# Value products of two heads alternate in one group per step, and the causal mask moves into the scan

## The chip, the cores and the metric

The kernel runs on one core of one Trainium2 chip. TensorE (PE, with its weight loads shown as PEld), VectorE (DVE), ScalarE (ACT), GpSimd (POOL) and the DMA queues work side by side and wait for each other through semaphores. The metric is the device time of one run in microseconds (us). The median of three runs of the kernel before is 3113.42 us (3112.48 to 3114.47).

## The reference

Two blocks follow each other on a sequence of 1024 rows with 1024 features. The first block has two layers (window attention, then a gated linear recurrence, each with memory attention and a wide MLP); nothing of it is touched. The second block has 8 stick-breaking heads and 8 sliding-window heads, each of width 64, between an input projection and an output projection. What the change touches is this part of the reference:

```
for start in range(0, S, BLOCK):            # BLOCK = 128 queries
    end = start + BLOCK
    z = einsum('bqhd,bkhd->bhqk', q[:, start:end], k[:, :end]) * scale
    causal = kpos < qpos
    log_beta = log_sigmoid(z)
    log_1mb = where(causal, log_sigmoid(-z), 0.0)
    later = cumsum(log_1mb, axis=3, reverse=True) - log_1mb
    w = where(causal, exp(log_beta + later), 0.0)
    outs.append(einsum('bhqk,bkhd->bqhd', w, v[:, :end]))
```

So the weight of key s for query t is sigmoid(z_ts) times the product of sigmoid(-z_tj) over the keys j between s and t, and zero for s at or after t.

## The kernel before, in words

The second block works on features in the partitions. `Piece.half` (L1147) computes one projected piece of 128 features for one half of the sequence: 24 matmuls of 128x512 into a PSUM bank `pj` of the tag "mm", which has two banks. The piece is then evacuated by ACT and DVE.

The 8 stick-breaking heads go in four pairs; the two heads of a pair (j = 0 and 1) lie in partitions 0 to 63 and 64 to 127. For each pair there are eight steps n = 0 to 7, one for each block of 128 queries, and step n has n + 1 blocks of keys. The loop is at L1291 to L1301. One turn of it writes down, in this order, the scores of step n + 1 (`sb_a`), one half of a projection that a later pair needs (`pc.half`), and the values of step n (`sb_b`).

`sb_a` (L1178): for each chunk of up to 512 keys and each head, three matmuls (L1193) that use 64 rows of the array, into a PSUM bank `z` of the tag "S", which has three banks. In the chunk that holds the diagonal a fourth matmul (L1196, bf16) adds a large negative number at keys that are not before the query. ACT makes `om` = sigmoid(-z/8) (L1197) and `be` = sigmoid(z/8) (L1198). DVE runs a product scan over `om` from the last key to the first (L1201), and `be` is multiplied by the scan shifted by one key (L1204; DVE for head 0, POOL for head 1). `be` has four buffers, which is two steps, and `om` has two, which is one step.

`sb_b` (L1207) takes one head after the other. For each head and each group of up to four key blocks it transposes `be` on PE (L1217) into a bank of the tag "tr" (two banks), copies it to an SBUF tile `wt` (three buffers; L1220 DVE for the first group, L1222 ACT for the second), and multiplies each block with the values (L1224): 128 rows, 64 columns of the array, output in `po` at partitions 64j to 64j + 63. So the products of head 0 occupy the array's columns 0 to 63 and those of head 1 columns 64 to 127. Each such product is two matmul instructions in the trace: 288 products, 576 instructions. `stage_out` (L1165) then multiplies with the gate and stores.

The sliding-window heads follow (L1304 to L1315) with `sw_a` and `sw_b` (L1253). `sw_b` handles two query blocks in one `po`; for each block it transposes and copies both heads together, then multiplies (L1271) the two key blocks of head 0 and the two of head 1.

The order of instructions on each engine is fixed when the program is built: the tile framework plays the program forward with assumed durations and takes, on each engine, the earliest written instruction whose inputs and buffers are there. `ahead(n)` (L94) makes it treat the instructions inside as if they had been written n instructions earlier. On the chip each engine then runs its list in that order and waits where a semaphore is not there yet.

Of the kernel before, what the change touches and what calls it, by code (L numbers as in the profile page):

```python
# [10 lines left out]

F32 = mybir.dt.float32
F32R = mybir.dt.float32r
BF16 = mybir.dt.bfloat16
I32 = mybir.dt.int32
AF = mybir.ActivationFunctionType
ALU = mybir.AluOpType
# [5 lines left out]
P = 128  # L23
D = 1024
S = 1024
# [5 lines left out]
NEG = -1e30  # L31
# [13 lines left out]


@with_exitstack
def net_kernel(ctx: ExitStack, tc: tile.TileContext, xT, memT, vecs, pos, sinks, invf, mask0, maskc, alibi,
               w_memk, w_memv, w_attn, w_mq, w_out, w_up, w_down, w_lru, w_gate, w_in2, w_out2, w_ada, outT):
    nc = tc.nc  # L50
    pe, act, dve, pool = nc.tensor, nc.scalar, nc.vector, nc.gpsimd

    cp = ctx.enter_context(tc.tile_pool(name="cp", bufs=1))
# [15 lines left out]
    psp = Tags(ctx.enter_context(tc.tile_pool(name="ps", bufs=1, space=PSUM)), {"mm": 2, "S": 3, "tr": 2, "po": 1})  # L69
# [13 lines left out]
    def nm(base):  # L83
        n_name[0] += 1
        return f"{base}_{n_name[0]}"

    ident = cp.tile([P, P], F32, tag="ident", name="ident")
# [356 lines left out]
    with tc.tile_pool(name="s0", bufs=1) as tp, \  # L444
# [19 lines left out]
        for l in range(2):  # L464
# [15 lines left out]
            for q in range(4):  # L480
                wh, wl = weight(w_memv[l * 4 + q])
                nc.sync.dma_start(xs[4 + q][:, hs(l)], xT[:, 4 + q, hs(l)])
                for m in range(2):
                    mm3(pss[m], [(memh[:, 2 * q + k, m * P:m * P + P], meml[:, 2 * q + k, m * P:m * P + P],
                                  wh[:, k * 512:k * 512 + 512], wl[:, k * 512:k * 512 + 512]) for k in range(2)],
                        start=q == 0, stop=q == 3)
# [47 lines left out]
    with ExitStack() as ph:  # L534
        a0, pre = side_pool(ph, "a0", "left"), ph.enter_context(ExitStack())
        a0r = side_pool(pre, "a0r", "right")
        T = Tags({"row": a0r, "rs": a0r, "ta": a0r, "tb": a0r, None: a0}, {"q": 12, "st": 12, "pt": 4, "mP": 1})
        gs = {}

        def proj_a(g, t):  # L540
            if g not in gs:
                gs[g] = ([weight(w_attn[g * 4 + q], 768) for q in range(4)],
                         T.tile([P, 2, S], F32R, "ks", nm("ks")), T.tile([P, NB, HD], F32, "vr", nm("vr")), [])
            ws, ks, vr, qs = gs[g]
# [3 lines left out]
                               ws[k // 2][1][:, (k % 2) * 384:(k % 2) * 384 + 384]) for k in range(KC)])  # L548
            row = T.tile([P, 384], F32, "row", nm("row"))
            act.copy(row, ps[:, :384])  # L550
# [3 lines left out]
            rsw = row[:, :320].rearrange("p (h a e) -> p h a e", a=8, e=8)[:, :, :2, :][:, :, ::-1, :]  # L554
            ta = T.tile([P, 5, 16], F32, "ta", nm("ta"))
            tb = T.tile([P, 5, 16], F32, "tb", nm("tb"))
# [300 lines left out]
    for l in range(2):  # L857
        if l == 1:

            with ExitStack() as ph:  # L860
# [3 lines left out]
                le = side_pool(lru, "a1", "left")  # L864
                T = Tags({"xb": ra, "xch": ra, "xcl": ra, "gl": rb, None: le},
                         {"xch": 1, "xcl": 1, "sq": 1, "i": 3, "r": 3})
# [99 lines left out]
                for c in range(KC):  # L966
# [3 lines left out]
                    ri = lru_g(c, cc[1], cc[2])  # L970
# [142 lines left out]
        down = ctx.enter_context(ExitStack())  # L1113


    identb = cp.tile([P, P], BF16, tag="identb", name="identb")
    dve.tensor_copy(identb, ident)
    mskc = cp.tile([P, P], BF16, tag="mskc", name="mskc")
    mskf = cp.tile([P, P], F32, tag="mskf", name="mskf")
    nc.scalar.dma_start(mskf, maskc)  # L1120
    dve.tensor_copy(mskc, mskf)
    with ExitStack() as ph:
        ri = ph.enter_context(tc.tile_pool(name="a2r", bufs=1, side="right", reuse_waits="tile"))
        le = side_pool(down, "a2", "left")
        T = Tags({"qkh": ri, "qkl": ri, "vr": ri, None: le}, {"qkh": 4, "qkl": 4, "be": 4, "st": 8, "wt": 3})

        def proj(w, th):
            wh, wl = w
# [49 lines left out]
        def sb_a(pc, n):  # L1178
            (qh, ql), (kh, kl) = pc[0].t, pc[1].t
            nk = (n + 1) * P  # L1180
            qs_ = slice(n * P, n * P + P)
            bes = [T.tile([P, S], F32, "be", nm("be")) for _ in range(2)]
            oms = [T.tile([P, S + 1], F32, "om", nm("om")) for _ in range(2)]
            for j in range(2):
                pool.memset(oms[j][:, nk:nk + 1], 1.0)
            for k0 in range(0, nk, 512):
                w = min(512, nk - k0)
                diag = k0 + w == nk
                zs = [psp.tile([P, 512], F32, tag="S", name=nm("z")) for _ in range(2)]
                for i, (a, b) in enumerate(((qh, kh), (qh, kl), (ql, kh))):  # L1190
                    for j in range(2):
                        rs_ = slice(64 * j, 64 * j + 64)
                        pe.matmul(zs[j][:, :w], a[rs_, qs_], b[rs_, k0:k0 + w], start=i == 0, stop=i == 2 and not diag)  # L1193
                for j in range(2):
                    if diag:
                        pe.matmul(zs[j][:, w - P:w], identb, mskc, start=False, stop=True)  # L1196
                    act.activation(oms[j][:, k0:k0 + w], zs[j][:, :w], AF.Sigmoid, scale=-0.125)  # L1197
                    act.activation(bes[j][:, k0:k0 + w], zs[j][:, :w], AF.Sigmoid, scale=0.125)  # L1198
            for j in range(2):
                be, om = bes[j], oms[j]  # L1200
                dve.tensor_tensor_scan(out=om[:, :nk][:, ::-1], data0=om[:, :nk][:, ::-1],  # L1201
                                       data1=om[:, :nk][:, ::-1], initial=1.0, op0=ALU.mult, op1=ALU.bypass)
                e = pool if j else dve
                e.tensor_tensor(out=be[:, :nk], in0=be[:, :nk], in1=om[:, 1:nk + 1], op=ALU.mult)  # L1204
            return bes

        def sb_b(pc, n, bes, st, chunk):  # L1207
            vr, sg = pc[2].t, pc[3].t
            po = psp.tile([P, HT], F32, tag="po", name=nm("po"))
            for j in range(2):  # L1210
                rs_ = slice(64 * j, 64 * j + 64)
                be = bes[j]
                for k0 in range(0, n + 1, 4):
                    kn = min(4, n + 1 - k0)
                    pt = psp.tile([P, 512], F32, tag="tr", name=nm("wtr"))
                    for b in range(kn):
                        pe.transpose(pt[:, b * P:b * P + P], be[:, (k0 + b) * P:(k0 + b + 1) * P], ident)  # L1217
                    wt = T.tile([P, 512], F32, "wt", nm("wt"))
                    if k0 == 0:
                        dve.tensor_copy(wt[:, :kn * P], pt[:, :kn * P])  # L1220
                    else:
                        act.copy(wt[:, :kn * P], pt[:, :kn * P])  # L1222
                    for b in range(kn):
                        pe.matmul(po[rs_, :P], vr[:, k0 + b, rs_], wt[:, b * P:b * P + P],  # L1224
                                  start=k0 + b == 0, stop=k0 + b == n, skip_group_check=True)
            stage_out(st, po, sg, chunk, n, P)

        def sw_a(pk, pq, c, n0, alb):
# [24 lines left out]
        def sw_b(pv, pg, c, n0, p, st):  # L1253
            vr, sg = pv.t, pg.t
            po = psp.tile([P, HT], F32, tag="po", name=nm("wpo"))
            for nn in range(2):
                n = n0 + nn
                k0 = max(0, n - 1)
                kb = n + 1 - k0
                pt = psp.tile([P, 512], F32, tag="tr", name=nm("swt"))  # L1260
                for j in range(2):
                    for b in range(kb):
                        o = (j * kb + b) * P
                        pe.transpose(pt[:, o:o + P], p[:, 2 * nn + j, b * P:b * P + P], ident)  # L1264
                wt = T.tile([P, 512], F32, "wt", nm("swp"))
                (act.copy if nn else dve.tensor_copy)(wt[:, :2 * kb * P], pt[:, :2 * kb * P])
                for j in range(2):
                    rs_ = slice(64 * j, 64 * j + 64)
                    for b in range(kb):
                        o = (j * kb + b) * P  # L1270
                        pe.matmul(po[rs_, nn * P:nn * P + P], vr[:, k0 + b, rs_], wt[:, o:o + P],  # L1271
                                  start=b == 0, stop=b == kb - 1, skip_group_check=True)
            stage_out(st, po, sg, 4 + c, n0, 256)

        KINDS = ("split", "split", "rows", "gate")
# [15 lines left out]
        for p in range(4):  # L1291
            st = [None, None]
# [11 lines left out]
        for c in range(4):  # L1304
            st = [None, None]
# [62 lines left out]
def layout(**inp):  # L1368
    a = {k: np.asarray(v) for k, v in inp.items()}
    o = {}  # L1370
# [13 lines left out]
    qi = np.arange(P)[:, None]  # L1384
    rel = np.arange(3 * P)[None, :] - P - qi
    o["mask0"] = np.where(np.abs(rel) <= 128, 0.0, 8 * NEG).astype(np.float32)
    o["maskc"] = np.where(np.arange(P)[None, :] < qi, 0.0, 8 * NEG).astype(np.float32)
    rel2 = P + qi - np.arange(2 * P)[None, :]
    tabs = []
    for c in range(4):  # L1390
# [39 lines left out]
    for c in range(4):  # L1430
# [6 lines left out]
    return {k: np.ascontiguousarray(v) for k, v in o.items()}  # L1437


ORDER = ("xT", "memT", "vecs", "pos", "sinks", "invf", "mask0", "maskc", "alibi", "w_memk", "w_memv", "w_attn", "w_mq",  # L1440
         "w_out", "w_up", "w_down", "w_lru", "w_gate", "w_in2", "w_out2", "w_ada")


# [17 lines left out]
```

## Time and profile before

| | |
|---|---|
| runs | 3113.42 us median of 3 (3112.48 to 3114.47) |
| profiled execution | 3114.57 us, its span 3112.6 us |
| granted TensorE clock, mean over the span | 0.981 |
| busy | PE 2994.6 us (96%), DVE 1803.7 (58%), ACT 1300.7 (42%), POOL 391.9 (13%) |
| stick-breaking stage | scores first at 2468.8 us, values last at 2892.3 us |

The busy time of an engine is the union of its instructions. Matmuls overlap in the array: a row that begins 0.23 us after the one before can still last 0.39 us. So how fast a group of matmuls passes is read from the starts, or from the length of a whole group, and not from the mean duration of one.

### The profile page before, as it was taken

How to read it: one execution, taken by the hardware profiler on the slowest of the kernel's cores; microseconds unless marked ns; L12 is line 12 of the kernel's file. 1: busy time of each engine (PE TensorE's matmuls, PEld its weight loads, DVE VectorE, ACT ScalarE, POOL GpSimd, SP SyncE). 2: the span in 40 equal slices, each digit the busy share in tenths (PEclk: the TensorE clock that was granted, in tenths of full speed). 3: DMA queues.
4: the chain of work that ended last, by engine and by line, in shares of the span. 5: the costliest groups of instructions: out<-in, count | busy, mean ns of one | idle time of the engine just before them, and what ended most of it. 6: DMA issues, size and time to landing. Idle time of an engine off the chain costs nothing. (4 is left out here: it accounts for less than half of the span.)

```text
span 3112.6 us, 38989 instructions
## 1 busy us (share of the span) xinstructions
PE 2994.6 (96%) x14688; PEld 2430.1 (78%) x14688; DVE 1803.7 (58%) x3071; ACT 1300.7 (42%) x2390; POOL 391.9 (13%) x426
## 2 busy tenths in 40 slices
PE   8999999799999999999889889999999899999998
PEld 7888778678888888777667768888888677777777
DVE  8666754774456542788764674445243745555555
ACT  6566541544542221366751444451121433334442
POOL 3222100300000000243310300000001201111102
PEclk9999999999999999999999989999999899999999
DMA  7111354343365432221263333354231210111142
GB/s 265 36 55 55 101 194 150 125 149 102 108 215 194 143 115 71 68 68 65 78 254 139 119 129 109 109 181 151 68 123 54 81 55 35 35 35 48 62 176 75
DMA packets 136348, 341.61 MB, mean 110 GB/s; under 512 B 14944, under 2 KB 29664, under 8 KB 136160
## 3 DMA queue, kind: packets, MB, share of 16 engines
q1 hardware_dynamic: 131840, 331.93, 31.1%
q10 hardware_dynamic: 4320, 7.20, 0.7%
q8 instruction: 115, 1.88, 0.2%
q14 instruction: 73, 0.60, 0.1%
HBM read 245.22 MB, written 93.85 MB: 109 GB/s over the span
## 5 line engine op out<-in xcount | busy, mean ns | idle before, releaser
L122 PE MATMUL psd<-uh,wh 128*128 128x512 f32 (+1 forms) x1568 | 606.2, 387 | 2.5 <-DVE mql L105 1.7
L126 PE MATMUL psd<-uh,wl 128*128 128x512 f32 (+1 forms) x1568 | 606.5, 387 | 0.0
L125 PE MATMUL psd<-ul,wh 128*128 128x512 f32 (+1 forms) x1568 | 606.3, 387 | 0.0
L104 ACT CAST wh<-wr 128x1024 fp32r<-128x1024 f32 (+2 forms) x236 | 234.7, 998 | 730.6 <-PE psd L125 506.3
L105 DVE TENSOR_TENSOR wl<-wr,wh 128x1024 fp32r<-128x1024 f32 (+2 forms) x260 | 314.4, 1212 | 218.1 <-ACT wh L104 216.9
L316 DVE TENSOR_TENSOR x<-x,psd 128x512 f32<-128x512 f32 x288 | 196.1, 685 | 377.7 <-PE psd L126 372.6
L122 PEld LDWEIGHTS psd<-uh,wh 128*128 128x128 f32 x1568 | 294.6, 188 | 63.8 <-issue 2.3
L126 PEld LDWEIGHTS psd<-uh,wl 128*128 128x128 f32 x1568 | 294.6, 188 | 60.7 <-issue 2.6
L125 PEld LDWEIGHTS psd<-ul,wh 128*128 128x128 f32 x1568 | 294.6, 188 | 59.7 <-issue 1.7
L122 PE MATMUL psu<-oph,wh 128*128 128x512 f32 x512 | 200.4, 394 | 41.1 <-ACT wh L104 41.1
L154 POOL TENSOR_TENSOR acc<-acc,sq 128x512 f32<-128x512 f32 (+1 forms) x70 | 95.8, 1369 | 1009.5 <-ACT sq L150 998.3
L125 PE MATMUL psu<-opl,wh 128*128 128x512 f32 x512 | 199.8, 391 | 0.0
L126 PE MATMUL psu<-oph,wl 128*128 128x512 f32 x512 | 198.6, 390 | 0.0
L125 PE MATMUL pj<-hl,wh 128*128 128x512 f32 x416 | 166.1, 404 | 8.0 <-DVE hl L105 8.0
L122 PE MATMUL pj<-hh,wh 128*128 128x512 f32 x416 | 168.4, 409 | 2.5 <-DVE qkl L105 1.3
L126 PE MATMUL pj<-hh,wl 128*128 128x512 f32 x416 | 167.0, 406 | 0.0
L122 PEld LDWEIGHTS psu<-oph,wh 128*128 128x128 f32 x512 | 96.6, 189 | 62.4 <-ACT wh L104 42.0
L125 PEld LDWEIGHTS psu<-opl,wh 128*128 128x128 f32 x512 | 96.7, 189 | 20.3 <-issue 0.5
L126 PEld LDWEIGHTS psu<-oph,wl 128*128 128x128 f32 x512 | 96.6, 189 | 20.3
L1201 DVE TENSOR_TENSOR_SCAN om<-om 128x128 f32<-128x128 f32 (+7 forms) x64 | 86.0, 1352 | 38.5 <-ACT om L1197 38.3
L122 PE MATMUL psx<-hh,wh 128*128 128x512 f32 x256 | 99.0, 397 | 4.8 <-ACT gl L897 4.8
L122 PE MATMUL psu<-oph,vh 128*128 128x512 f32 x256 | 100.7, 393 | 0.0
(337 smaller groups left out, 6027.9 us busy)
## 6 DMA issues: line engine op xcount, KB each, us to landing
wr<-in_w_up SPq DMA_DIRECT2D x64, 512.0 KB, 3.8
ud<-cc SPq DMA_DIRECT2D x128, 256.0 KB, 2.2
ur<-ud SPq DMA_DIRECT2D x64, 512.0 KB, 3.4
wr<-in_w_down SPq DMA_DIRECT2D x64, 512.0 KB, 4.1
wr<-in_w_out SPq DMA_DIRECT2D x32, 512.0 KB, 3.6
wr<-in_w_in SPq DMA_DIRECT2D x26, 512.0 KB, 3.5
wra<-in_w_ada SPq DMA_DIRECT2D x24, 512.0 KB, 4.3
uh<-mixh SPq DMA_DIRECT2D x20, 512.0 KB, 7.6
```

The source lines that it names most:

```text
L104: act.copy(hi, src)
L105: lo_eng.tensor_tensor(out=lo, in0=src, in1=hi.bitcast(F32), op=ALU.subtract)
L122: ins = pe.matmul(out, lh, rh, start=start and i == 0, stop=False, skip_group_check=skip)
L125: pe.matmul(out, lh, rl, start=False, stop=False, skip_group_check=skip)
L126: ins = pe.matmul(out, ll, rh, start=False, stop=stop and i == n - 1, skip_group_check=skip)
L154: pool.tensor_tensor(out=self.acc[:, :n], in0=self.acc[:, :n], in1=sq[:, :n], op=ALU.add)
L316: dve.tensor_tensor(out=xs, in0=xs, in1=ps, op=ALU.add)
L1201: dve.tensor_tensor_scan(out=om[:, :nk][:, ::-1], data0=om[:, :nk][:, ::-1], data1=om[:, :nk][:, ::-1], initial=1.0, op0=ALU.mult, op1=ALU ...
```

## The change

Four edits. The mask matmul, its two constants and the input that it came from go; the scan gets a second operand `turns` that is zero but for an identity matrix in the diagonal block, and adds it after the multiplication, from 0 at the start: the running product is 0 before the diagonal, becomes 1 at it and is multiplied from there on. The element beyond the last key is set to 0 and not 1. The second chunk's scores of head 1 use a bank of the tag "mm" and not "S". In `sb_b` all transposes and copies of a step come first (the copies of head 0 on DVE, of head 1 on ACT, `wt` now with five buffers), and then all products of both heads in one group, from the last key block to the first, the heads alternating, written 200 instructions ahead. `sw_b` is turned the same way.

```diff
-        T = Tags({...}, {"qkh": 4, "qkl": 4, "be": 4, "st": 8, "wt": 3})
+        T = Tags({...}, {"qkh": 4, "qkl": 4, "be": 4, "st": 8, "wt": 5, "turns": 1})
+        turns = T.tile([P, S], F32, "turns", nm("turns"))
+        pool.memset(turns[:, :S - P], 0.0)
+        pool.tensor_copy(turns[:, S - P:], ident)
...
-                pool.memset(oms[j][:, nk:nk + 1], 1.0)
+                pool.memset(oms[j][:, nk:nk + 1], 0.0)
...
-                zs = [psp.tile([P, 512], F32, tag="S", name=nm("z")) for _ in range(2)]
+                zs = [psp.tile([P, 512], F32, tag="mm" if k0 and j else "S", name=nm("z")) for j in range(2)]
...
-                    if diag:
-                        pe.matmul(zs[j][:, w - P:w], identb, mskc, start=False, stop=True)
...
-                                       data1=om[:, :nk][:, ::-1], initial=1.0, op0=ALU.mult, op1=ALU.bypass)
+                                       data1=turns[:, S - nk:][:, ::-1], initial=0.0, op0=ALU.mult, op1=ALU.add)
...  sb_b
-            for j in range(2):
-                for k0 in range(0, n + 1, 4):
...
-                    for b in range(kn):
-                        pe.matmul(po[rs_, :P], vr[:, k0 + b, rs_], wt[:, b * P:b * P + P],
-                                  start=k0 + b == 0, stop=k0 + b == n, skip_group_check=True)
+            for k0 in range(0, n + 1, 4):
+                for j in range(2):
...
+                    (act.copy if j else dve.tensor_copy)(wt[:, :kn * P], pt[:, :kn * P])
+                    wts.append(wt)
+            with ahead(200):
+                for b in range(n, -1, -1):
+                    for j in range(2):
+                        rs_ = slice(64 * j, 64 * j + 64)
+                        pe.matmul(po[rs_, :P], vr[:, b, rs_], wts[b // 4 * 2 + j][:, b % 4 * P:b % 4 * P + P],
+                                  start=b == n, stop=b == 0, skip_group_check=True)
...  sw_b
+            with ahead(200):
+                for nn in (1, 0):
+                    wt, k0, kb = wts[nn]
                     for b in range(kb):
-                        o = (j * kb + b) * P
+                        for j in range(2):
+                            o = (j * kb + b) * P
```

## Rows read from the trace of the kernel before

**Rows 1.** Page, busy time of the engines and busy tenths in 40 slices.
```profile
PE 2994.6 (96%) x14688; PEld 2430.1 (78%) x14688; DVE 1803.7 (58%) x3071; ACT 1300.7 (42%) x2390; POOL 391.9 (13%) x426
...
PE   8999999799999999999889889999999899999998
```

**Rows 2.** Busy time by stretch: start:end us, length, busy us (instructions), clock, DMA share.
```profile
2460.00:2895.00 435.00, 433.59 (x2300) 321.96 (x2300) 243.78 (x370) 165.68 (x360) 51.88 (x102) 0.99 0.13 43
2895.00:3113.00 218.00, 205.62 (x1266) 164.56 (x1264) 117.17 (x339) 89.17 (x223) 36.42 (x50) 0.97 0.31 109
```

**Rows 3.** Chain that ended last, stretch 2460 to 2895 us, shares by line.
```profile
by line: PE pj L122 17.4%; PE pj L126 17.2%; PE pj L125 17.2%; PE po L1224 15.7%; PE z L1193 14.7%; PE wtr L1217 9.1%; PE z L1196 2.1%; PE vtr L1158 1.2%; issue 1.2%; PE ws L1243 1.0%; POOL hr L252 0.8%; ACT hr L260 0.5%; DVE qkl L105 0.4%;
```

**Rows 4.** Groups by line, whole run: count | busy us, mean ns | idle before, releaser.
```profile
L1224 PE MATMUL po<-wt,vr 128*64 128x128 f32 x576 | 73.0, 279 | 0.0
L1217 PEld LDWEIGHTS wtr<-ident,be 128*128 128x128 f32 x288 | 31.7, 140 | 10.9 <-issue 9.1 <-DVE be L1204 0.4
L1196 PE MATMUL z<-mskc,identb 128*128 128x128 bf16 x64 | 13.8, 229 | 0.0
L1271 PE MATMUL wpo<-swp,vr 128*64 128x128 f32 x240 | 18.2, 283 | 0.0
```

**Rows 5.** PE in order of time: start us, us of the group, line, tiles, count.
```profile
2526.72 0.44 PE L1224 MATMUL po<-wt,vr 128*64 128x128 f32 x4
...
2636.64 0.66 PE L1224 MATMUL po<-wt,vr 128*64 128x128 f32 x8
...
2678.95 1.09 PE L1224 MATMUL po<-wt,vr 128*64 128x128 f32 x8
...
2701.12 0.39 PE L122 MATMUL pj<-hh,wh 128*128 128x512 f32 x1
2701.35 0.39 PE L125 MATMUL pj<-hl,wh 128*128 128x512 f32 x1
2701.67 1.96 PE L1224 MATMUL po<-wt,vr 128*64 128x128 f32 x16
...
2910.36 1.14 PE L1271 MATMUL wpo<-swp,vr 128*64 128x128 f32 x16
```

**Rows 6.** Groups by line and shape: the scores of 512 keys, first of three terms.
```profile
L1193 PE MATMUL z<-qkh,qkh 64*128 64x512 f32 x48 | 21.8, 495 | 0.0
```

**Rows 7.** PE in order of time: scores of two heads together, and of one head.
```profile
2643.32 0.50 PE L1193 MATMUL z<-qkh,qkh 64*128 64x512 f32 x2
2643.66 0.40 PE L1193 MATMUL z<-qkl,qkh 64*128 64x512 f32 x2
2643.89 0.41 PE L1193 MATMUL z<-qkh,qkl 64*128 64x512 f32 x2
2644.14 0.28 PE L1193 MATMUL z<-qkh,qkh 64*128 64x256 f32 x1
...
2711.68 0.49 PE L1193 MATMUL z<-qkh,qkh 64*128 64x512 f32 x1
2712.01 0.39 PE L1193 MATMUL z<-qkl,qkh 64*128 64x512 f32 x1
2712.24 0.39 PE L1193 MATMUL z<-qkh,qkl 64*128 64x512 f32 x1
2712.57 0.23 PE L1196 MATMUL z<-mskc,identb 128*128 128x128 bf16 x1
2712.61 0.47 PE L125 MATMUL pj<-hl,wh 128*128 128x512 f32 x1
```

**Rows 8.** Waits, stretch 2460 to 2895 us: us in total, times, longest us.
```profile
ACT be L1198 <- PE wtr L1217: 46.6, 16, 5.9
```

**Rows 9.** Groups by line and shape: copies to `wt` and the longest scan, 2460 to 2895 us.
```profile
L1220 DVE COPY wt<-wtr 128x512 f32<-128x512 f32 x40 | 27.4, 685 | 33.6 <-PE wtr L1217 33.4
L1201 DVE TENSOR_TENSOR_SCAN om<-om 128x1024 f32<-128x1024 f32 x8 | 18.3, 2290 | 7.4 <-ACT om L1197 7.4
L1222 ACT COPY wt<-wtr 128x512 f32<-128x512 f32 x8 | 4.7, 586 | 21.9 <-PE wtr L1217 21.9
```

**Rows 10.** A scan in the first block that multiplies and adds: count, ns min/median/max, start us.
```profile
L947 DVE TENSOR_TENSOR_SCAN r<-a,i x8: 2274/2277/2283, 1347.6 to 1575.9; 128x1024 f32<-128x1024 f32 x8
```

More of the change, by code (lines that the diff above doesn't have):

```diff
@@ L13 @@
 F32R = mybir.dt.float32r
-BF16 = mybir.dt.bfloat16
 I32 = mybir.dt.int32
@@ L47, in net_kernel @@
 @with_exitstack
-def net_kernel(ctx: ExitStack, tc: tile.TileContext, xT, memT, vecs, pos, sinks, invf, mask0, maskc, alibi,
+def net_kernel(ctx: ExitStack, tc: tile.TileContext, xT, memT, vecs, pos, sinks, invf, mask0, alibi,
                w_memk, w_memv, w_attn, w_mq, w_out, w_up, w_down, w_lru, w_gate, w_in2, w_out2, w_ada, outT):
@@ L1113, in net_kernel @@
         down = ctx.enter_context(ExitStack())
[L1116 to L1121, printed above, removed]
     with ExitStack() as ph:
@@ L1124, in net_kernel @@
         le = side_pool(down, "a2", "left")
-        T = Tags({"qkh": ri, "qkl": ri, "vr": ri, None: le}, {"qkh": 4, "qkl": 4, "be": 4, "st": 8, "wt": 3})
+        T = Tags({"qkh": ri, "qkl": ri, "vr": ri, None: le}, {"qkh": 4, "qkl": 4, "be": 4, "st": 8, "wt": 5, "turns": 1})
+        turns = T.tile([P, S], F32, "turns", nm("turns"))
+        pool.memset(turns[:, :S - P], 0.0)
+        pool.tensor_copy(turns[:, S - P:], ident)
         def proj(w, th):
@@ L1184, in sb_a @@
             for j in range(2):
-                pool.memset(oms[j][:, nk:nk + 1], 1.0)
+                pool.memset(oms[j][:, nk:nk + 1], 0.0)
             for k0 in range(0, nk, 512):
                 w = min(512, nk - k0)
-                diag = k0 + w == nk
-                zs = [psp.tile([P, 512], F32, tag="S", name=nm("z")) for _ in range(2)]
+                zs = [psp.tile([P, 512], F32, tag="mm" if k0 and j else "S", name=nm("z")) for j in range(2)]
                 for i, (a, b) in enumerate(((qh, kh), (qh, kl), (ql, kh))):
@@ L1192, in sb_a @@
                         rs_ = slice(64 * j, 64 * j + 64)
-                        pe.matmul(zs[j][:, :w], a[rs_, qs_], b[rs_, k0:k0 + w], start=i == 0, stop=i == 2 and not diag)
+                        pe.matmul(zs[j][:, :w], a[rs_, qs_], b[rs_, k0:k0 + w], start=i == 0, stop=i == 2)
                 for j in range(2):
-                    if diag:
-                        pe.matmul(zs[j][:, w - P:w], identb, mskc, start=False, stop=True)
                     act.activation(oms[j][:, k0:k0 + w], zs[j][:, :w], AF.Sigmoid, scale=-0.125)
@@ L1209, in sb_b @@
             po = psp.tile([P, HT], F32, tag="po", name=nm("po"))
-            for j in range(2):
-                rs_ = slice(64 * j, 64 * j + 64)
-                be = bes[j]
-                for k0 in range(0, n + 1, 4):
-                    kn = min(4, n + 1 - k0)
+            wts = []
+            for k0 in range(0, n + 1, 4):
+                kn = min(4, n + 1 - k0)
+                for j in range(2):
                     pt = psp.tile([P, 512], F32, tag="tr", name=nm("wtr"))
                     for b in range(kn):
-                        pe.transpose(pt[:, b * P:b * P + P], be[:, (k0 + b) * P:(k0 + b + 1) * P], ident)
+                        pe.transpose(pt[:, b * P:b * P + P], bes[j][:, (k0 + b) * P:(k0 + b + 1) * P], ident)
                     wt = T.tile([P, 512], F32, "wt", nm("wt"))
[L1219 to L1222, printed above, removed]
-                    for b in range(kn):
-                        pe.matmul(po[rs_, :P], vr[:, k0 + b, rs_], wt[:, b * P:b * P + P],
-                                  start=k0 + b == 0, stop=k0 + b == n, skip_group_check=True)
+                    (act.copy if j else dve.tensor_copy)(wt[:, :kn * P], pt[:, :kn * P])
[6 more added lines that the diff above has]
+                                  start=b == n, stop=b == 0, skip_group_check=True)
             stage_out(st, po, sg, chunk, n, P)
@@ L1255, in sw_b @@
             po = psp.tile([P, HT], F32, tag="po", name=nm("wpo"))
+            wts = []
             for nn in range(2):
@@ L1266, in sw_b @@
                 (act.copy if nn else dve.tensor_copy)(wt[:, :2 * kb * P], pt[:, :2 * kb * P])
-                for j in range(2):
-                    rs_ = slice(64 * j, 64 * j + 64)
+                wts.append((wt, k0, kb))
+            with ahead(200):
+                for nn in (1, 0):
+                    wt, k0, kb = wts[nn]
                     for b in range(kb):
-                        o = (j * kb + b) * P
-                        pe.matmul(po[rs_, nn * P:nn * P + P], vr[:, k0 + b, rs_], wt[:, o:o + P],
-                                  start=b == 0, stop=b == kb - 1, skip_group_check=True)
+                        for j in range(2):
+                            rs_ = slice(64 * j, 64 * j + 64)
+                            o = (j * kb + b) * P
+                            pe.matmul(po[rs_, nn * P:nn * P + P], vr[:, k0 + b, rs_], wt[:, o:o + P],
+                                      start=b == 0, stop=b == kb - 1, skip_group_check=True)
             stage_out(st, po, sg, 4 + c, n0, 256)
@@ L1386, in layout @@
     o["mask0"] = np.where(np.abs(rel) <= 128, 0.0, 8 * NEG).astype(np.float32)
-    o["maskc"] = np.where(np.arange(P)[None, :] < qi, 0.0, 8 * NEG).astype(np.float32)
     rel2 = P + qi - np.arange(2 * P)[None, :]
@@ L1437, in layout @@
     return {k: np.ascontiguousarray(v) for k, v in o.items()}
-ORDER = ("xT", "memT", "vecs", "pos", "sinks", "invf", "mask0", "maskc", "alibi", "w_memk", "w_memv", "w_attn", "w_mq",
+ORDER = ("xT", "memT", "vecs", "pos", "sinks", "invf", "mask0", "alibi", "w_memk", "w_memv", "w_attn", "w_mq",
          "w_out", "w_up", "w_down", "w_lru", "w_gate", "w_in2", "w_out2", "w_ada")
```

## The prediction

> **What bounds the kernel now.** I read the page's busy times first: PE is busy for 96% of the span, and the slices of the second block (the last quarter) show it at 9 tenths throughout [rows 1]. A busy PE isn't yet a PE at its peak, so the next view is the busy time by stretch. The stick-breaking stage runs from 2460 to 2895 us. PE is busy for 433.6 of its 435 us at a granted clock of 0.99, DVE for 243.8 (56%), ACT for 165.7 and POOL for 51.9 [rows 2]. The reader is to see that PE has no gap here and that no other engine is near its limit. The third view is the chain that ended last in this stretch: 52% of it are projections (three rows of 17%), 15.7% the value products, 14.7% the scores, 9.1% the transposes and 2.1% the mask matmuls; no other engine has more than 1% [rows 3]. So in this stage a microsecond that PE doesn't need is a microsecond off the span, as long as the other engines keep up. In the transposes, PE waited for `be` for 0.4 us in all [rows 4]: the scan and its multiplication are done long before they are needed. In the last 218 us PE is busy for 205.6 [rows 2], so what is won before 2895 us isn't waited away behind it.
>
> **The products.** The 576 product instructions take 73.0 us together [rows 4]. How fast a group passes depends on whose they are. Sixteen instructions of one head (step 7) take 1.96 us, and eight of one head 1.09: (1.96 - 1.09)/8 = 0.109 us for each more. Eight of both heads (step 1: two products of head 0, two of head 1) take 0.66 us, and sixteen in `sw_b`, where the heads change every two products, 1.14: (1.14 - 0.66)/8 = 0.060 us for each more [rows 5]. The two heads use different columns of the array, and where both are at hand they evidently run side by side. In the new order a step is one group of 4(n + 1) instructions with the heads alternating. With 0.44 us for the four of step 0, 0.66 for eight, and 0.06 for each more, the eight steps take 0.44 + 0.66 + 0.90 + 1.14 + 1.38 + 1.62 + 1.86 + 2.10 = 10.1 us, and four pairs 40.4. Against 73.0 that is **-32.6 us**. The bounds: nothing, if one head's products have all passed before the other's copy is there; and -36 if the slope is the 0.0545 that half of 0.109 would be. I take -32.6, since the copy of head 1 (ACT, 0.586 us for 512 columns) ends at most a few products behind that of head 0 (DVE, 0.685) [rows 9].
>
> The Trainium skill has a rule against this: "TensorE: Matmul & The Clock Gate", section "The mechanism", says that a weight load overlaps a running matmul only when its row group differs, and that matmuls start and end strictly in order. The two heads share all 128 rows and differ in columns; by that rule nothing would overlap, and the term would be zero. The trace disagrees: 1.14 us against 1.96 for the same sixteen instructions [rows 5].
>
> **Groups and their borders.** Each change of the array's shape costs something. Projections begin 0.23 us apart, but the first product behind one begins 0.32 us after it (2701.35 to 2701.67) [rows 5]: 0.09 us at the entry that no group's own length holds. The code has one group per head and step, 64 in all, and will have 32; the 32 entries saved are **-3 us**, between 0 (where the heads stood together already) and -6 (if an exit costs as much).
>
> **The mask.** 64 bf16 matmuls with a busy time of 13.8 us [rows 4], much of it beside others: a mask begins 0.33 us after the last score (0.10 more than the 0.23 between scores), and the projection behind it 0.04 us later [rows 7], and a border to the projection stays. Bounds -2.6 (64 x 0.04) and -13.8; I take **-6**, near the chain's 2.1% of 435 = 9.1 [rows 3], less the border that remains. The constants' load and copies go from DVE and ACT's queue; they are not on the path.
>
> **The scan.** It reads a second tile and adds. The 1024-element scan takes 2290 ns now [rows 9]; one that multiplies and adds with two tiles, in the first block, 2277 [rows 10]. Zero, bounds from -1 to +1 us over 64 scans, and in any case on DVE, which has 44% of the stage free. The memset and copy of `turns` are two POOL instructions on an engine with 52 of 435 us in use [rows 2]: zero; if a tile's space came free late they would hold up the first scans by a few us at the most, and projections are there to fill.
>
> **The scores.** The diff doesn't speak of it, but the spare bank and the new order should bring the heads' scores together as well. Now the first terms of 512 keys, 48 of 495 ns (23.8 us if none overlapped), have a union of 21.8 [rows 6]; full pairing would halve it, so a sixth is paired. A pair of 512 keys takes 0.82 us (2643.32 to 2644.14), one head alone 0.89 (2711.68 to 2712.57) [rows 7]: pairing saves 0.96 us each time. There are 24 chunks of 512 keys, of which 20 aren't paired (19 us), and 8 each of 384, 256 and 128, worth 9 us by their widths (8 x 0.96 x 768/512, five sixths of it). So 0 to -28. For it: four banks at hand for the four scores of steps 4 to 7, where there were three, and `be` buffers of both heads that come free together, since their transposes now stand together. Against: the heads' sigmoids still free the first bank before the second. I take 40%: **-12 us**.
>
> **What is added.** The products stand 200 instructions ahead, so they are taken as soon as the copies are expected, and where a copy is late PE stands. Before, they came after the projection and had no such wait. At worst each of 32 steps waits for a copy, 0.585 us: +19; at best nothing. I take **+5**. Queued behind a waiting product are the projection's matmuls and the next scores, which is why it costs PE directly. Copies move from DVE to ACT (16 of 64), which has 62% of the stage free. `sw_b` overlaps already [rows 5], so its turn is worth about a microsecond either way: zero.
>
> **Sum.** -32.6 - 3 - 6 - 12 + 5 = -48.6 us, from the profiled execution's 3114.57 to 3066; that execution is 1.2 us above the median of the runs, so **3065 us**. The likeliest case's own range is 3045 to 3085.
>
> **Rivals.**
> (1) The products don't run side by side: the planner takes head 0's products while head 1's copy is on its way, and the group becomes two halves of one head each, or the weights of one head are not loaded while the other's product runs. The second is what the rule of the Trainium skill above says. For it: most of the groups of both heads in the trace of before are such halves. Against: a copy takes 0.6 to 0.7 us [rows 9] and head 1's is on another engine, while step 7 has 3.5 us of products (32 x 0.109). The product term is then 0, the pairing of scores half: 3114.6 - 3 - 6 - 6 + 5 = 3105 us.
> (2) Scores pair fully, the mask's borders go as a whole and nothing waits: -32.6 - 4 - 9 - 27 = -73, so 3041 us.
> (3) The slower side: the bank from "mm". Scores of head 1 hold it until their sigmoids are done, and ACT waits for a `be` buffer before them: 16 waits, 46.6 us, longest 5.9 [rows 8]. Projections have two "mm" banks. If in each of the 16 steps 4 to 7 the next projection needs the one that is held or the one not yet evacuated, PE loses its filler. At the mean wait of 2.9 us that is +47, which eats the gain (3113); at the longest, +94: 3159. It decides from 48.6/16 = 3.0 us a step. Against: the projections and the scores take the banks in turn, so the other one is mostly free, and transposes, products and scores of the neighbouring steps lie between two projections.
> (4) PE's saving turns into a wait for the scan chain. DVE would have 244 of 386 us, 63%. Against: 0.4 us of waits for `be` in all. Not more than 10 us back: inside the range.
>
> **How the numbers follow.** The forecast gets 0.62, rival 1 0.14, rival 2 0.15, rival 3 0.07 (half of it slower, half near no change, with another 0.02 for mishaps in the order that the planner finds for the rest). Four fifths of that lie between **3036 and 3099**: from somewhat past rival 2 to just short of rival 1. About 0.2% (6 us) is what a measurement of this kernel can tell from no change. Faster by more: 0.90; within: 0.04; slower: 0.06.
>
> **What would show it.** Right: 576 product instructions in 32 groups with a union near 40 us; no mask rows; the scores' union of 512 keys nearer 15 than 22 us; the scan at 2.29 us; PE still without gaps, and sw_b unchanged. Wrong: product groups of one head each with 0.109 us a piece; projections that begin after a wait for ACT or DVE; PE rows that name `wt` copies as releasers for more than 10 us.

## The result and the profile after

The changed kernel takes 3063.47 us (median of 4, 3062.59 to 3064.53) against 3113.72 (median of 4, 3112.48 to 3114.47): a ratio of 0.9839, 95% interval 0.9822 to 0.9856. That is 50 us off; 48.6 were forecast, with 3065 us as the time. Its profiled execution took 3062.59 us with a span of 3060.8.

The page of the changed kernel, busy times and PE's slices, as [rows 1]:

```profile
PE 2936.4 (96%) x14624; PEld 2395.3 (78%) x14624; DVE 1793.7 (59%) x3053; ACT 1308.9 (43%) x2408; POOL 395.1 (13%) x428
...
PE   8999999989999999998889979999999999999998
```

PE is as full as before, with 64 instructions less and 58 us less of busy time; 55 of these lie in the stick-breaking stage and 3 before 2460 us, where the code is unchanged. The stretches that answer to [rows 2] show where:

```profile
2460.00:2843.00 383.00, 378.41 (x2237) 288.59 (x2237) 233.95 (x359) 172.03 (x384) 54.35 (x104) 0.99 0.15 50
2843.00:3061.00 218.00, 205.56 (x1269) 165.47 (x1267) 118.63 (x336) 90.48 (x218) 36.71 (x50) 0.97 0.31 109
```

The stick-breaking stage went from 435 to 383 us, and the last 218 us took 218 again. These borders are round numbers. From the first score to the end of the last value product it is 424.0 us before (2468.8 to 2892.7) and 368.6 in the changed kernel (2469.2 to 2837.8), and what follows took 219.9 and takes 223.1: 17 projection matmuls have moved there from the stage (949 of 966 are left in it). PE has 4.6 us of gaps in the stretch where it had 1.4. DVE is at 61% of the shorter stage. The chain in the first of these stretches, as [rows 3]:

```profile
by line: PE pj L121 19.8%; PE pj L124 19.0%; PE pj L125 18.5%; PE z L1188 11.5%; PE po L1217 10.7%; PE wtr L1209 8.8%; issue 1.6%; PE vtr L1154 1.5%; PE ws L1236 1.2%; POOL hr L251 0.9%; ACT wt L1211 0.7%; DVE om L1194 0.7%; DVE qkl L104 0.
```

Products fell from 15.7% of 435 us (68) to 10.7% of 383 (41), scores from 14.7% (64) to 11.5% (44), and the masks' 2.1% (9) is gone. The groups by line say the same, count | busy us, mean ns | idle before; the second row is the scores' first term of 512 keys, which answers to [rows 6]:

```profile
L1217 PE MATMUL po<-wt,vr 128*64 128x128 f32 x576 | 46.2, 280 | 0.8 <-DVE wt L1211 0.8
L1188 PE MATMUL z<-qkh,qkh 64*128 64x512 f32 x48 | 16.6, 494 | 0.5 <-ACT be L1191 0.5
L1209 PE MATMUL wtr<-ident,be 128*128 128x128 f32 x288 | 46.0, 280 | 1.0 <-ACT wt L1211 1.0
L1269 PE MATMUL wpo<-swp,vr 128*64 128x128 f32 x240 | 16.9, 280 | 0.2 <-ACT swp L1260 0.2
L1194 DVE TENSOR_TENSOR_SCAN om<-om,turns 128x1024 f32<-128x1024 f32 x8 | 18.1, 2281 | 2.1 <-ACT om L1190 2.1
```

PE in order of time: first a step whose group is split, then a whole one, and scores of two heads together in between (start us, us of the group, line, tiles, count):

```profile
2604.43 0.43 PE L1217 MATMUL po<-wt,vr 128*64 128x128 f32 x2
2604.79 0.33 PE L1209 MATMUL wtr<-ident,be 128*128 128x128 f32 x1
2605.05 1.96 PE L1217 MATMUL po<-wt,vr 128*64 128x128 f32 x30
...
2613.18 0.50 PE L1188 MATMUL z<-qkh,qkh 64*128 64x512 f32 x2
2613.52 0.40 PE L1188 MATMUL z<-qkl,qkh 64*128 64x512 f32 x2
2613.75 0.40 PE L1188 MATMUL z<-qkh,qkl 64*128 64x512 f32 x2
2614.08 0.50 PE L124 MATMUL pj<-hl,wh 128*128 128x512 f32 x1
...
2681.47 1.97 PE L1217 MATMUL po<-wt,vr 128*64 128x128 f32 x32
```

The 32 instructions of step 7 pass in 1.97 us; 16 took 1.96 before [rows 5]. But in the step at 2604.43 one product (two instructions) of head 0 went before the others, with a transpose between. A group, here and below, is a run of product matmuls on PE with no other matmul between them.

### The profile page after: what moved, and what is told of

It is laid out like the page before. It is cut to its first block, busy times and chain, and to the rows that moved or that the text cites. A ratio compares the mean times of both kernels' runs of the same rounds, so it can differ in the third digit from the quotient of the medians.

```text
span 3060.8 us, 38811 instructions
## 1 busy us (share of the span) xinstructions
PE 2936.4 (96%) x14624; PEld 2395.3 (78%) x14624; DVE 1793.7 (59%) x3053; ACT 1308.9 (43%) x2408; POOL 395.1 (13%) x428
## 5 line engine op out<-in xcount | busy, mean ns | idle before, releaser
L124 PE MATMUL psu<-opl,vh 128*128 128x512 f32 x256 | 100.6, 393 | 0.0
```

The lines of the kernel that those rows point to most:

```text
L124: pe.matmul(out, lh, rl, start=False, stop=False, skip_group_check=skip)
```

## The experiments

All are told by the median of their runs, with the ratio and its 95% interval, against 3113.9 us of the kernel before timed along with them. The theory: three savings of PE time, namely products side by side because they use different columns of the array, scores side by side, and no mask matmuls.

**Parts alone on the kernel before.**

```diff
mask_only:   mask matmul out, scan with turns and add; all else as before
group_only:  the new sb_b and "wt": 5; all else as before
bank_only:
-  zs = [psp.tile([P, 512], F32, tag="S", name=nm("z")) for _ in range(2)]
+  zs = [psp.tile([P, 512], F32, tag="mm" if k0 and j else "S", name=nm("z")) for j in range(2)]
```

> The kernel before with the mask edit alone (mask matmuls out, scan with turns; products, banks and sw_b as before). Theory (three separate savings: products side by side, scores side by side through the bank, mask matmuls out): 6 us off, 3107 to 3108, scan of 1024 at 2.28 to 2.29 us, product union still 73, union of the first score terms of 512 keys still near 22. Rival (the mask's borders held the heads' scores apart, so the mask edit brings the pairing): 15 to 20 us off, 3095, and that union at 17.

> The kernel before with the new sb_b alone (all copies first, products of both heads in one group written 200 ahead, wt with five buffers; mask matmuls, banks and sw_b as before). Theory: 26 us off for the products and 3 for borders, 3084 to 3087, product union near 46. Rival (copies that now stand on the path take part of it back): 3095 or more, with idle time of PE on wt copies above 10 us. Rival (the copies come free together and pair the scores too): 3070 to 3075, first score terms of 512 keys at 17.

> The kernel before with one edit: the second chunk's scores of head 1 in a bank of the tag mm. Theory: the missing fourth bank held the heads' scores apart, so 10 to 15 us off, 3099 to 3103, first score terms of 512 keys at 17 instead of 21.8. Rival (the scores pair because the be buffers come free together in the new sb_b): no change, 3113, 21 to 22. Rival of the prediction (the projection waits for its bank): slower, 3120 or more.

Measured: mask edit alone 3097.83 us (0.9952, 0.9937 to 0.9966), group alone 3078.58 (0.9887, 0.9872 to 0.9902), bank alone 3104.71 (0.9970, 0.9960 to 0.9979). So 16, 35 and 9 us, 60 together, where the whole change (with `sw_b`) has 50, and 45 without its `sw_b` edit (no_sw, below). The union of all scores (L1193, or L1188 in mask_only) from 2460 to 2900 us explains two thirds of the difference of 15. The rows are those of the kernel before, mask_only, group_only and bank_only, one fence each; behind the length, busy us (count) of PE, then PEld:

```profile
2460.00:2900.00 440.00, 71.97 (x288) 39.65 (x288) 0.99 0.13 44
```
```profile
2460.00:2900.00 440.00, 59.73 (x288) 33.62 (x288) 0.99 0.14 47
```
```profile
2460.00:2900.00 440.00, 63.52 (x288) 35.70 (x288) 0.99 0.15 49
```
```profile
2460.00:2900.00 440.00, 62.54 (x288) 36.18 (x288) 0.99 0.14 46
```

Each of the three edits alone takes 8 to 12 us off the scores, 30 added up, and all together 20 (52.10 in the changed kernel): part of the same saving is found more than once. The other 5 us were not traced. My theory had put the pairing down to the bank and the buffers; for the mask it had said 6 us, and the rival (15 to 20) was right. group_only came out between its theory and its second rival, bank_only 2 us above its theory. In group_only the products' union is 47.5, in mask_only and bank_only 71.4 and 71.7, so only the new `sb_b` touches the products.

**Scores tied, on the kernel before.** Within a chunk of keys every score matmul is tied behind the one written before it, head 1 first.

```diff
+  lead = None
   for i, (a, b) in enumerate(((qh, kh), (qh, kl), (ql, kh))):
-      for j in range(2):
+      for j in (1, 0):
-          pe.matmul(zs[j][:, :w], ...)
+          ins = pe.matmul(zs[j][:, :w], ...)
+          lead = pin(ins, lead) if lead else ins
```

> The kernel before with one edit: every score matmul is tied behind the one written before it, so that the heads' scores alternate (mask matmuls, banks, sb_b and sw_b as before). Theory (the pairing of the scores is a saving of its own, whichever edit brings it): scores from 65 to 50 or less of PE time, 12 to 16 us off, 3098 to 3102. Rival (pairing without the other edits makes PE wait for the third and fourth bank): 3108 or more, with PE idle before scores.

Measured: 3099.29 us (0.9952, 0.9937 to 0.9967), 14.6 off with nothing but an order. The scores' union is 55.20 us:

```profile
2460.00:2900.00 440.00, 55.20 (x288) 28.36 (x288) 0.99 0.15 48
```

So pairing is a saving by itself, as the theory said. The row of the first terms alone doesn't show it, since the tied heads overlap across the terms; it is where it was before [rows 6]:

```profile
L1194 PE MATMUL z<-qkh,qkh 64*128 64x512 f32 x48 | 22.3, 486 | 0.2 <-ACT be L1200 0.2
```

So the sign that the prediction gave for pairing, this row alone, was a poor one; the union of all scores tells it.

**A control.** The kernel before with five `wt` buffers and nothing else.

> The kernel before with five wt buffers in place of three, nothing else: a control for what any new order is worth. Theory (mask, bank and group each let the scores pair by what they do): 3110 to 3115, scores 62 to 66 us of PE time, no change in the products. Rival (the kernel before stood in an unlucky order of the planner, and any disturbance pairs the scores): 8 us or more off, 3106 or less, scores at 58.

Measured: 3113.42 us (0.9999, 0.9989 to 1.0008), products 73.0 and first score terms 21.8, as in [rows 4] and [rows 6]. The order of all 14688 matmuls came out as it was, so the run says that the buffers alone are worth nothing; whether any disturbed order would pair the scores it can't say.

**What makes the products fast.** First the changed kernel with head 0's products before head 1's within the group; then with the alternation kept but both heads in the same 64 columns (head 1's results land beside head 0's in the bank, and its values are left out of the output).

```diff
heads_in_turn:
-  for b in range(n, -1, -1):
-      for j in range(2):
+  for j in range(2):
+      for b in range(n, -1, -1):
same_columns:
-  pe.matmul(po[rs_, :P], vr[:, b, rs_], wts[...]...
+  pe.matmul(po[:64, j * P:j * P + P], vr[:, b, rs_], wts[...]...
```

> The changed kernel, but inside the group all products of head 0 come before those of head 1; the group, its place 200 ahead, the banks and the mask edit stay. Theory (products run side by side only where the heads alternate closely): 24 to 27 us slower than the changed kernel, 3087 to 3090, product union near 70. Rival (the saving is one group in place of two, and the order inside doesn't matter): 3063 to 3066, product union near 46.

> The changed kernel, but the products of head 1 use the same 64 columns of the array as head 0 (they land beside head 0's in the bank; the values of head 1 that reach the output are left out). Order, group and waits as in the changed kernel. Theory (products of two heads run side by side because they occupy different columns): nothing overlaps, 0.109 us from start to start, product union 66 to 70, 3080 to 3088. Rival (the alternation itself, two output regions or two wt tiles, makes the pace): 46 and 3063 to 3066.

Measured: heads in turn 3074.52 us (0.9876, 0.9861 to 0.9890), same columns 3092.52 (0.9930, 0.9913 to 0.9946). Their product rows, heads in turn first:

```profile
L1217 PE MATMUL po<-wt,vr 128*64 128x128 f32 x576 | 64.1, 278 | 0.8 <-DVE wt L1211 0.8
```
```profile
L1221 PE MATMUL po<-wt,vr 128*64 128x128 f32 x576 | 74.7, 277 | 1.4 <-DVE wt L1215 1.4
```

With the same columns the products don't run side by side: no two of the 576 instructions start less than 0.109 us apart, where in the changed kernel they start in pairs, 7 ns apart, and the pairs 0.109 us. The union is 74.7 us against 46.2, and there are 29 us more of run time for 28.5 of union. Time and union lie above what I had expected; the order has 55 groups and not 50, which may be a part of it. So it is the columns; the PSUM partitions that the results go to change with them, and no run tells the two apart. Heads in turn still overlap by some 10 us (64.1 and not 74.7), and the run was 11 us slower than the changed kernel where I had expected 24 to 27: its scores are at 49.57 us of union (52.10 in the changed kernel), there are 43 groups and not 50, and head 1 begins while head 0 is still at work (last section). The alternation by itself is worth less than I thought.

**Parts taken out of the changed kernel.** The bank back to "S"; the products without the 200 ahead; `sw_b` as before.

> The changed kernel with the second chunk's scores of head 1 back in a bank of the tag S. Theory after the first runs (each edit by itself brought 8 to 9 us of pairing, together 15): scores take 5 to 8 us more PE time than in the changed kernel, 3068 to 3072. Rival (with the new order the bank is no longer needed): 3063 to 3065, scores as in the changed kernel. Products unchanged at a union near 46 in both.

> The changed kernel with the products of sb_b where they are written and not 200 instructions ahead. Theory (the alternation makes the pace, the place only decides when the group runs): 3060 to 3067, product union 44 to 47. Rival (the place holds the group together; without it projections and scores fall between the products): 3070 or more, over 60 product groups.

> The changed kernel with sw_b as before. Theory (its heads ran side by side already): 0 to 2 us slower, 3063 to 3066, sw_b's product union 17 to 18.5. Rival (its new group saves borders and waits as in sb_b): 4 us or more slower, 3067 or more.

Measured: no_bank 3076.30 us (0.9880, 0.9866 to 0.9895), scores' union 60.73; no_ahead 3062.70 (0.9838, 0.9821 to 0.9854), product union 45.3; no_sw 3068.69 (0.9856, 0.9841 to 0.9870), its runs from 3065.18 to 3071.85. The bank is worth 13 us in the new order, more than alone and more than the 5 to 9 that I had expected; 8.6 of it is the scores' union and 2.1 the products' (48.3). The place 200 ahead is worth nothing that can be measured. The turn of `sw_b`, which I had put at zero, is worth about 5 us in the new order, as its rival said; its product row in no_sw, against 16.9 in the changed kernel:

```profile
L1264 PE MATMUL wpo<-swp,vr 128*64 128x128 f32 x240 | 18.7, 290 | 0.0
```

That is 1.8 us. All of the difference lies behind the last stick-breaking product: that part takes 228.1 us in no_sw and 223.1 in the changed kernel, with the same matmuls. In the kernel before, with the old `sw_b` and 17 projection matmuls fewer, it took 219.9. So the old `sw_b` costs 5 us in the new order; in the old one at most 1, with 4 us counted for the 17. Where the other 3 of the 5 lie wasn't traced further.

**One group a step.** Head 1 first in each block, and head 0's first product tied behind head 1's first; then the scores tied as well.

```diff
+  lead = None
   for b in range(n, -1, -1):
-      for j in range(2):
+      for j in (1, 0):
+          ins = pe.matmul(po[rs_, :P], ...)
+          if b == n:
+              lead = pin(ins, lead) if lead else ins
```

> The changed kernel with head 1 first in each block and head 0's first product tied behind head 1's first, so that no product leaves ahead of its group. Theory (18 of the 50 product groups are a single product of head 0 that went when its copy was there and head 1's was not; each costs its own 0.22 us and a border): 32 groups, product union 41, 5 us faster, 3058 to 3060. Rival (the early product filled time in which PE had to wait for head 1's copy): the same time as the changed kernel, with idle time of PE before the products on the ACT copy of 4 us or more.

> As pin_first, and every score matmul tied behind the one written before it, so that the two heads' scores alternate strictly. Theory (scores that alternate run side by side; in the changed kernel half still don't): scores from 50 to about 40 us of PE time, first terms of 512 keys near 12.5, 3046 to 3052. Rival (waiting for both heads' banks makes PE stand or moves the scores too late): no faster than pin_first, with PE idle before scores or transposes.

Measured: pin_first 3057.57 us (0.9819, 0.9804 to 0.9833; runs 3055.7 to 3059.3), pin_all 3057.62 (0.9821, 0.9806 to 0.9835). The product row of pin_first, then that of pin_all with its transposes:

```profile
L1218 PE MATMUL po<-wt,vr 128*64 128x128 f32 x576 | 38.5, 278 | 0.0
```
```profile
L1211 PE MATMUL wtr<-ident,be 128*128 128x128 f32 x288 | 45.7, 280 | 2.9 <-DVE wt L1213 2.5 <-ACT wt L1213 0.4
...
L1220 PE MATMUL po<-wt,vr 128*64 128x128 f32 x576 | 38.5, 278 | 0.0
```

32 groups and 38.5 us: 7.7 less than the changed kernel, and 6 us of run time, with no wait before the products. The scores' union is 2.4 lower as well (49.69), so not all of the 6 need be the group. The runs of pin_first lie wholly below those of the changed kernel, though the two were timed at different times; with pin_all it is the fastest version here. Tying the scores too brought their union to 47.46 from 49.69 but no time: transposes now wait 2.9 us for copies. The expected 3046 to 3052 wasn't reached, and the scores stayed at 47 us of PE where I had said 40.

## Why the prediction was right, point by point

Unions overlap each other, so their differences don't add up to the run time. The time from each matmul's start to the next start on PE, with PE's idle time taken off, does. Worked out from the two traces, from the first score to the last value product, it is in us:

| | before | changed | difference | forecast |
|---|---|---|---|---|
| value products | 68.5 | 42.7 | -25.8 | -32.6 |
| scores | 65.4 | 47.9 | -17.5 | -12 |
| mask matmuls | 4.4 | 0 | -4.4 | -6 |
| transposes of `be` | 39.3 | 36.7 | -2.6 | in the borders' -3 |
| projections | 236.3 (966) | 227.7 (949) | -8.6 | in the borders' -3 |
| other matmuls | 8.6 | 9.1 | +0.5 | |
| PE idle | 1.3 | 4.5 | +3.2 | +5 |
| the stage | 424.0 | 368.6 | -55.4 | |
| what follows it | 219.9 | 223.1 | +3.2 | 0 |

The 17 projection matmuls that moved are worth 4.1 us at 0.245 us each, so like for like the projections won 4.5 us and what follows the stage 0.9.

**What bounds.** Right. The gain is in the stick-breaking stage and is PE time; behind it all but about 1 us is work that moved.

**Products: -32.6 forecast, -26.8 measured (73.0 to 46.2).** The mechanism was right: same_columns takes all of it back. The size was off because the group isn't one group in every step: the planner often puts the first product of head 0 on PE's list as soon as it expects its copy. Counted in the trace there are 50 groups, not 32, and 21 of them are a single product. With 32 (pin_first) the union is 38.5, 34.5 off. The price of 0.060 us was a little high too: 4 instructions take 0.44 us and 32 take 1.97, which is 0.0546 for each more, half of 0.109. It had come from groups where the heads change only every two products. At 0.0546 the prediction's own sum gives -34.4 and not the -36 that it names as its bound, and pin_first reaches it. So the step that was mis-sized is the number of groups. I had seen that head 1's copy ends later and thought of its effect on the alternation, not on the group.

**Borders: -3 forecast, about -7 measured.** With 14 groups fewer (64 to 50) it would be 14 x 0.09 = 1.3 us by the same price. But the projections won 4.5 us like for like and the transposes 2.6, so this term was too small, beyond its bound of -6. Which borders these are, of products, scores or masks, wasn't taken apart.

**Mask: -6 forecast, -4.4 measured.** That is the time up to the next start that is gone with its rows, without borders. In mask_only it is 16 us in all, but 12.2 of them are the pairing of the scores that it brought.

**Scan: zero.** 2281 ns for 1024 elements, 2290 before [rows 9]. But two of the 64 scans ran long in the changed kernel, one of 640 elements with 2.60 us (the seven others 1.47 to 1.49) and one of 128 with 1.81 (0.40 to 0.43); in the kernel before and in mask_only none did. The cause stays open.

**Scores: -12 forecast, -17.5 measured, -19.9 in union (71.97 to 52.10).** The reason that I gave held for the bank (8.6 us of the scores' union in no_bank) and missed the mask. By the chain's shares it is 64 to 44 us. This term was too small by 5 to 8.

**Waits: +5 forecast.** PE's gaps in the stage grew by 3.2 us (1.4 to 4.6). They are, in the changed kernel (us in total, times, longest us):

```profile
PE pj L121 <- DVE qkl L104: 2.2, 2, 1.9
...
PE wtr L1209 <- ACT wt L1211: 1.0, 2, 0.5
...
PE po L1217 <- DVE wt L1211: 0.8, 2, 0.4
...
PE z L1188 <- ACT be L1191: 0.5, 2, 0.3
```

The 1.9 us stand at the start of the stage, where there were 1.3 before; only 0.8 are the waits of products for copies that the term was made of.

**`sw_b`: zero forecast, about -1 against the kernel before.** This is what the part behind the stage won like for like. That the old form would cost 5 us in the new order (no_sw) I hadn't seen: I had looked at whether its products overlap, not at its borders and order.

So the sum was right to 2 us (by the profiled executions, which lie 52.0 apart, to 3) because the terms' errors cancel: the savings of products and mask were put 8 us too high, those of scores and borders 10 too low, and waits and `sw_b` came out 3 better than assumed. That the mechanism was right is shown; that the time came out to 2 us is luck. Rival 1 (heads don't run side by side) fell with the 32 instructions in 1.97 us, and with it the rule of the Trainium skill, "TensorE: Matmul & The Clock Gate", section "The mechanism", that a weight load overlaps a running matmul only where its row group differs: the trace disagrees for columns, 46.2 us against 74.7 with shared ones. That matmuls start strictly in order, which the prediction quotes beside it, fails here too (last section). The other half of rival 1, products of head 0 taken early, came true for single products. Rival 2 (everything pairs) came true only in part: even with the scores tied the time was 3057.6 and not 3041. Rival 4 (the scan chain) cost next to nothing: no wait of PE in the stage names the multiplication of `be` (L1197). The long scan of 640 elements does stand on the chain, at 2696.84 us, and DVE's work queued behind it leaves PE idle for 0.34 us before a projection at 2702.76. Rival 3 (projections waiting for the bank) fell with bank_only, which is 9 us faster. Of the signs of being right, the 32 groups and the union near 40 us came only with pin_first.

What stays open: why each single edit lets the planner pair the scores. The runs show that it does, and that tying them does it too; they don't show which of its choices turned.

## What to carry to other kernels

Where two matmuls of half the array's columns are at hand, write them so that they follow each other closely: here that halved the time of each further instruction of a product, from 0.109 to 0.055 us, and it shows as starts in pairs and not in the mean duration (279 ns before, 280 in the changed kernel). When an edit moves matmuls, count the groups and the pairs of everything that shares the engine: about a third of the stage's gain (17.5 of 55.4 us) came from scores that the diff hardly names. Where a planner orders the instructions, one whose input comes early can be put ahead of its group; where a group matters, tie its first member to the one whose input comes last.

## What the runs showed of the hardware that wasn't expected

Products of two heads overlap in part even where all of one head's are queued before the other's: 64.1 us of union in heads_in_turn against 74.7 where the columns are shared. A step 7 of heads_in_turn, as one group of 32 instructions:

```profile
2610.75 3.33 PE L1217 MATMUL po<-wt,vr 128*64 128x128 f32 x32
```

One after the other they would take 1.96 + 16 x 0.109 = 3.70 us [rows 5], alternating 1.97. In the starts of this group the first four instructions of head 1 pass beside the last four of head 0 and the rest one by one, which is the 0.4 us that it is shorter. The trace doesn't name the head of an instruction; this is read from the pitch: twelve starts one by one, 0.109 us apart (0.160 after the first), then two starts 6 ns apart, at 1.361 us into the group, then six about 55 ns apart, and the rest 0.109 us apart again. The same holds in all 20 groups of this run that hold both heads and eight instructions or more, of 8 to 32: head 1 begins beside the fourth instruction from the end of head 0. So a matmul did start before earlier ones of the other columns, but over four instructions and no more. This fits that only a close alternation pairs the whole group; what sets the four the runs don't show.
